# Gate and up projections of a decoder block by Strassen's seven products

## The chip, the cores and the metric

The kernel runs on one core of one Trainium2 chip. The metric is the device time of one execution in microseconds (us), the median of several runs. TensorE multiplies matrices, VectorE and ScalarE (in the rows DVE and ACT) work element by element, GpSimd is POOL, and SyncE (SP) issues the transfers from DRAM.

## The reference, cut to what matters

A decoder block with attention and convolution branches is followed by a SwiGLU feed-forward layer and a final norm, for 512 tokens of width 1,024; `D_FF` is 2,816. The change is in the feed-forward layer:

```python
    x = x + merged @ w_out
    h = rms_norm(x, norm_ffn_g)
    x = x + (jax.nn.silu(h @ w_ffn_gate) * (h @ w_ffn_up)) @ w_ffn_down
return rms_norm(x, norm_final_g)
```

All in float32.

## The kernel before

Every product of this part is made of three: each float32 operand is split into `hi`, its value rounded to the type F32R that TensorE takes, and `lo`, the rest, and `mm3` adds hi x hi, hi x lo and lo x hi into one PSUM bank. The weights are split on the fly. `wload` fetches two k tiles of 128 rows x 256 columns in one transfer of 256 KB (256 columns of float32, 1,024 bytes a row) into a tile `wr`; ScalarE casts it to `wh` (L136), and in this part VectorE subtracts to `wl` (L137). The pool of weights has six buffers each of `wr`, `wh` and `wl`, 128 x 512 elements a buffer.

The normalized input h is held transposed, channels on the partitions, as eight pairs `h2_hi[k]`, `h2_lo[k]` of 128 x 512 (channels x tokens). `h2_T` makes them for one half of the tokens at a time: TensorE transposes, ScalarE writes hi (L1034), VectorE writes lo (L1035).

Gate and up go chunk by chunk: eleven chunks of 256 columns of the 2,816. `ffn_chunk` does, for gate and then for up, two column halves m of 128, each with eight k tiles, with the weights as the stationary operand and 512 tokens as the moving one. At the end of a gate half ScalarE takes Silu out of PSUM (tile `sil`, L1059); at the end of an up half VectorE multiplies (L1065), ScalarE casts to `a_hi` (L1066) and VectorE subtracts to `a_lo` (L1067). Chunk 0 is done in two halves of 256 tokens, so that it can begin before the second half of h is transposed.

The down projection (tile `pd`) reads `a_hi` and `a_lo` as stationary operands, with `w_ffn_down` loaded by `wload_wide` (L147 to L149): first the left 512 output columns, all 22 k tiles for four token tiles; then the right 512, where the last `nl` = 8 k tiles are done token tile by token tile, each followed by its norm and its store.

A planner (the Tile framework) orders the instructions of each engine at compile time: among those that its own timing finds ready, the one that stands earlier in the program goes first. So the order on an engine can differ from that of the program, and is fixed in the compiled kernel. `tile_pool` hands out buffers by tag, `bufs` of each; an instruction that writes a buffer waits until the last reader of its former content is done.

Of the kernel before, what the change touches and what calls it, by code (L numbers as in the profile page):

```python
# [19 lines left out]
D = 1024  # L20
# [16 lines left out]
def hybrid_block(  # L37
# [72 lines left out]

    WG = 2

    def wload_raw(src, k0, nk, c0, ncol):

        pieces = []
        for a in range(0, nk, WG):
            n = min(WG, nk - a)
            raw = wp.tile([128, WG, 256], F32, name="wr", tag="wr", bufs=6)
# [6 lines left out]
    def wload(src, k0, nk, c0, ncol, pieces=None, on_dve=None, tile=None):  # L125

        on_dve = phase["lo_dve"] if on_dve is None else on_dve
        eng = nc.vector if on_dve else nc.gpsimd
        tile = tile or (lambda name: wp.tile([128, WG, 256], F32R, name=name, tag=name))
        res = []  # L130
        for raw, n in pieces or wload_raw(src, k0, nk, c0, ncol):
            hi, lo = tile("wh"), tile("wl")
            st = n if phase["early"] else min(n, 2)
            for a in range(0, n, st):
                sl = slice(a, min(a + st, n))
                nc.scalar.copy(hi[:, sl, :ncol], raw[:, sl, :ncol])  # L136
                eng.tensor_sub(lo[:, sl, :ncol], raw[:, sl, :ncol], hi[:, sl, :ncol].bitcast(F32))  # L137
            res += [(hi[:, j, :], lo[:, j, :]) for j in range(n)]
        return res

    def wload_wide(src, k, c0, ncol=512, parts=()):

        wide = [wp.tile([128, WG, 256], dt, name=n, tag=n, bufs=6 if n == "wr" else None)
                .rearrange("p a b -> p (a b)") for n, dt in (("wr", F32), ("wh", F32R), ("wl", F32R))[:3 - len(parts)]]
# [869 lines left out]

    hp = ctx.enter_context(tc.tile_pool(name="hid", bufs=16))
    for t in range(2, NT):
# [10 lines left out]

    def h2_T(th, hh):
        for k in range(KT):
            p = trp("th2")  # L1030
            for j in range(2):
# [19 lines left out]
    gfin = fp.tile([128, D], F32, name="gfin")  # L1051
    nc.gpsimd.dma_start(gfin, norm_final_g[None, :].to_broadcast([128, D]))

    def ffn_chunk(c, n0, n1):
        sgs = []

        def ev_g(m, p):
            s_ = fp.tile([128, S], F32, name="sil", tag="sil", bufs=3)
            nc.scalar.activation(s_[:, n0:n1], p[:, n0:n1], AF.Silu)  # L1059
            sgs.append(s_)  # L1060

        def ev_u(m, p):
            f = 2 * c + m
            s_ = sgs[m][:, n0:n1]
            nc.vector.tensor_mul(s_, p[:, n0:n1], s_)  # L1065
            nc.scalar.copy(a_hi[f][:, n0:n1], s_)  # L1066
            nc.vector.tensor_sub(a_lo[f][:, n0:n1], s_, a_hi[f][:, n0:n1].bitcast(F32))  # L1067

        for src, ev in ((w_ffn_gate, ev_g), (w_ffn_up, ev_u)):
            p = [dense("pf") for _ in range(2)]  # L1070
            for kh in range(2):
                ws = wload(src, 4 * kh, 4, 256 * c, 256)
                for m in range(2):
                    for kk in range(4):
# [31 lines left out]

    nl = 8
    pd = [dense("pd") for _ in range(NT)]
# [61 lines left out]
```

## Time and profile before

| | us |
|---|---|
| median of 3 runs (lowest to highest) | 971.59 (970.38 to 972.0) |
| profiled execution, its own time | 974.84 |
| its span, first to last instruction | 973.1 |
| TensorE busy | 940.4 (97%) |
| VectorE busy | 633.1 (65%) |
| ScalarE busy | 545.1 (56%) |
| gate and up chunks | from 601.8 to 845.3 |
| down projection to the end | from 845.3 to 973.1 |

The device time is that of the whole execution and is a little over the span. Busy times are sums of the durations on an engine; matmuls overlap each other, so their rate is read from their starts.

### The profile page before, as it was taken

What the parts mean: (1) busy time and instruction counts of PE and PEld (TensorE: products, weight loads), DVE (VectorE), ACT (ScalarE), POOL (GpSimd) and SP (SyncE); (2) the same over time, 40 slices, a digit from 0 to 9 for tenths busy, and PEclk for the clock granted to TensorE, in tenths of its full rate; (3) what the DMA queues carried; (4) which work ended last, traced back from release to release, by engine and by line L of the source; (5) the groups of instructions that cost most, each with busy time, mean ns of one, the idle gap of its engine ahead of it and who ended that gap; (6) DMA issues with size and microseconds to landing.
All of it is one profiled execution on the core that took longest, in us unless ns stands there. A gap on an engine that the chain in (4) does not pass through costs nothing.

```text
span 973.1 us, 14959 instructions
## 1 busy us (share of the span) xinstructions
PE 940.4 (97%) x5306; PEld 797.5 (82%) x5306; DVE 633.1 (65%) x1254; ACT 545.1 (56%) x1273; POOL 234.9 (24%) x256
## 2 busy tenths in 40 slices
PE   5999989899999999989999999999999999999996
PEld 5889979888888977877778878988888888888886
DVE  6799999987999987676876877633333343322512
ACT  6533545558879887999984776533333333322412
POOL 3545447853353342622322000000000000000000
PEclk9999989999999999999999999999999999999999
DMA  7333324542121111111212166633333323322302
GB/s 225 90 106 88 87 72 121 134 109 55 45 66 44 34 45 44 44 33 55 98 56 76 59 201 188 180 96 100 91 105 88 107 87 108 97 96 95 118 29 87
DMA packets 77599, 89.03 MB, mean 91 GB/s; under 512 B 5896, under 2 KB 65620, under 8 KB 77524
## 3 DMA queue, kind: packets, MB, share of 16 engines
q1 hardware_dynamic: 76676, 87.38, 30.0%
q8 instruction: 42, 0.69, 0.3%
q0 software_dynamic: 144, 0.52, 0.2%
q14 instruction: 33, 0.27, 0.1%
q10 hardware_dynamic: 704, 0.17, 0.1%
HBM read 85.96 MB, written 2.10 MB: 90 GB/s over the span
## 4 chain that ended last, share of the span: by engine, by line
PE 85%; DVE 7%; ACT 4%; issue 1%; DMA 1%; POOL 1%; SPq 0%; POOLq 0%; ACTq 0%; DVEq 0%
PE pf L211 8%; PE pf L212 8%; PE pf L213 8%; PE pch L213 7%; PE pch L211 7%; PE pch L212 7%; PE ptk L211 4%; PE ptk L212 4%; PE ptk L213 4%; PE pd L211 4%; PE pd L213 4%; PE pd L212 4%; PE tP L732 3%; PE sc L700 2%; PE sc L701 2%; PE pv L756 2%
## 5 line engine op out<-in xcount | busy, mean ns | idle before, releaser
L137 POOL TENSOR_TENSOR wl<-wr,wh 128x512 fp32r<-128x512 f32 x128 | 167.2, 1318 | 229.8 <-ACT wh L136 179.5
L136 ACT CAST wh<-wr 128x512 fp32r<-128x512 f32 x228 | 140.1, 622 | 145.0 <-PE pf L212 52.6
L794 DVE SCALAR_TENSOR_TENSOR cacc<-z,cw,cacc 128x512 f32<-128x512 f32 x232 | 165.5, 748 | 3.8 <-ACT cacc L792 1.7
L211 PE MATMUL pf<-h2hi,wh 128*128 128x512 f32 (+1 forms) x384 | 142.3, 372 | 0.6 <-ACT h2hi L1034 0.6
L212 PE MATMUL pf<-h2lo,wh 128*128 128x512 f32 (+1 forms) x384 | 142.5, 372 | 0.0
L213 PE MATMUL pf<-h2hi,wl 128*128 128x512 f32 (+1 forms) x384 | 142.4, 372 | 0.0
L137 DVE TENSOR_TENSOR wl<-wr,wh 128x512 fp32r<-128x512 f32 x100 | 68.7, 689 | 109.6 <-ACT wh L136 108.1
L213 PE MATMUL pch<-hThi,wl 128*128 128x512 f32 (+1 forms) x272 | 107.3, 395 | 1.5 <-POOL wl L137 1.5
L211 PE MATMUL pch<-hThi,wh 128*128 128x512 f32 (+1 forms) x272 | 107.3, 396 | 1.2 <-ACT hThi L195 1.2
L212 PE MATMUL pch<-hTlo,wh 128*128 128x512 f32 (+1 forms) x272 | 107.5, 396 | 0.0
L149 DVE TENSOR_TENSOR wl<-wr,wh 128x512 fp32r<-128x512 f32 x76 | 51.6, 689 | 61.9 <-ACT wh L148 61.8
L148 ACT CAST wh<-wr 128x512 fp32r<-128x512 f32 (+1 forms) x84 | 50.1, 604 | 73.7 <-PE pd L213 50.9
L708 ACT ACTIVATE P<-sc,nm 128x32 f32<-128x32 f32 (+3 forms) x192 | 84.7, 446 | 11.2 <-DVE nm L705 9.2
L1136 POOL TENSOR_TENSOR rstd<-rstd,half 128x1 f32<-128x1 f32 x4 | 2.2, 547 | 359.6 <-DVE rstd L1135 359.6
L211 PEld LDWEIGHTS pf<-h2hi,wh 128*128 128x128 f32 x384 | 72.0, 188 | 13.2 <-ACT h2hi L1034 0.8
L211 PE MATMUL ptk<-wh,hThi 128*128 128x256 f32 x288 | 82.7, 287 | 0.0
L213 PEld LDWEIGHTS pf<-h2hi,wl 128*128 128x128 f32 x384 | 72.2, 188 | 12.6
L212 PEld LDWEIGHTS pf<-h2lo,wh 128*128 128x128 f32 x384 | 72.2, 188 | 12.4
L212 PE MATMUL ptk<-wl,hThi 128*128 128x256 f32 x288 | 81.2, 282 | 0.0
L213 PE MATMUL ptk<-wh,hTlo 128*128 128x256 f32 x288 | 81.0, 281 | 0.0
L705 DVE TENSOR_REDUCE nm<-sc 128x1 f32<-128x32 f32 (+3 forms) x192 | 68.8, 381 | 16.8 <-PE sc L703 15.5
L211 PE MATMUL pd<-wh,ahi 128*128 128x512 f32 (+1 forms) x184 | 70.0, 380 | 0.8 <-DVE x L1092 0.8
(234 smaller groups left out, 2133.0 us busy)
## 6 DMA issues: line engine op xcount, KB each, us to landing
wr<-in_w_in_dram SPq DMA_DIRECT2D x100, 256.0 KB, 2.8
wr<-in_w_ffn_gate_dram SPq DMA_DIRECT2D x48, 256.0 KB, 2.7
wr<-in_w_ffn_up_dram SPq DMA_DIRECT2D x48, 256.0 KB, 2.7
wr<-in_w_ffn_down_dram SPq DMA_DIRECT2D x44, 256.0 KB, 2.5
wr<-in_w_out_dram SPq DMA_DIRECT2D x32, 256.0 KB, 2.6
x<-in_x_dram SPq DMA_DIRECT2D x8, 512.0 KB, 5.0
wr<-in_w_conv_out_dram SPq DMA_DIRECT2D x16, 256.0 KB, 2.7
wr<-in_cmp_k_w_dram SPq DMA_DIRECT2D x8, 256.0 KB, 2.6
```

Of the source, the lines that this page charges most:

```text
L136: nc.scalar.copy(hi[:, sl, :ncol], raw[:, sl, :ncol])
L137: eng.tensor_sub(lo[:, sl, :ncol], raw[:, sl, :ncol], hi[:, sl, :ncol].bitcast(F32))
L148: nc.scalar.copy(hi, raw)
L149: (nc.vector if phase["lo_dve"] else nc.gpsimd).tensor_sub(lo, raw, hi.bitcast(F32))
L211: nc.tensor.matmul(o, lh, rh, start=first, stop=False, skip_group_check=True)
L212: nc.tensor.matmul(o, lh, rl, start=False, stop=False, skip_group_check=True)
L213: nc.tensor.matmul(o, ll, rh, start=False, stop=last, skip_group_check=True)
L700: nc.tensor.matmul(sc[:, :e - a], qh[:, tsl], K[:, a:e], start=True, stop=False)
L705: nc.vector.tensor_reduce(out=nm[:, b:b + 1], in_=sc[:, ba - a:be - a], axis=AX.X, op=OP.max, negate=True)
L708: nc.scalar.activation(P[:, ba:be], sc[:, ba - a:be - a], AF.Exp, bias=nm[:, b:b + 1], accum_out=Dn[:, b, hh:hh + 1])
L732: nc.tensor.transpose(t4[:, 256 * b + 128 * hh:256 * b + 128 * hh + 128], Ps[hh][:, key_blk(j, b)], idn)
L794: nc.vector.scalar_tensor_tensor(cts[c] if j == TAPS - 1 else a, z[:, j:j + S], cw[:, j, c:c + 1], a, op0=OP.mult, op1=OP.add)
```

## The change

Chunks 2 to 10 are no longer done by `ffn_chunk` but by `pair`, which uses Strassen's scheme in the form of Winograd: a product of two by two blocks takes seven products of blocks and some sums. The blocks of the weights are the k halves (512 rows) by the column halves (128 columns) of a chunk, gate and up side by side in a tile `quad` of 128 x 1,024: a11, a12, a21, a22. The blocks of h are k halves by token halves of 256. The four sums of weights (s1 to s4) are made on VectorE before the split into hi and lo. The four combinations of h (t1 to t4) are made once, in `combine`, during chunks 0 and 1. A product is 24 matmuls of 256 columns: gate in the left half of a PSUM bank, up in the right one. The results are put together with additions on VectorE (`total`) and copies out of PSUM on ScalarE (`saved`).

Other edits: the hidden activations are kept in float32 (`a_`), and their split into hi and lo moves into the first half of the down projection; the full float32 h (`full`) and the combinations live in tiles of `a_` that are written late; after chunk 1 the pool of weights is closed and opened again with three buffers each of `wh`, `wl` and `ws`, twice as large; `gfin` is loaded after the pairs; `nl` goes from 8 to 5; `pd` takes two of its banks from another tag.

The diff, its core:

```diff
-    hp = ctx.enter_context(tc.tile_pool(name="hid", bufs=16))
+    hp = ctx.enter_context(tc.tile_pool(name="hid", bufs=32))
...
+            if full:
+                nc.scalar.activation(full[k][:, sl], p[:, :256], AF.Copy, scale=g_ffn[:, k:k + 1])
...
-    a_hi = [fp.tile([128, S], F32R, name=f"ahi{f}") for f in range(FT)]
-    a_lo = [fp.tile([128, S], F32R, name=f"alo{f}") for f in range(FT)]
+    def a_tile(name, dt=F32):
+        return fp.tile([128, S], dt, name=name, tag="A", bufs=FT + 1)
+
+    a_ = [a_tile(f"a{f}") for f in range(FT)]
...
+    full, comb = a_[6:14], a_[14:22]
+    quads = ctx.enter_context(tc.tile_pool(name="quads", bufs=3))
...
-            s_ = fp.tile([128, S], F32, name="sil", tag="sil", bufs=3)
+            s_ = fp.tile([128, S], F32, name="sil", tag="saved", bufs=2)
...
-            nc.vector.tensor_mul(s_, p[:, n0:n1], s_)
-            nc.scalar.copy(a_hi[f][:, n0:n1], s_)
-            nc.vector.tensor_sub(a_lo[f][:, n0:n1], s_, a_hi[f][:, n0:n1].bitcast(F32))
+            nc.vector.tensor_mul(a_[2 * c + m][:, n0:n1], p[:, n0:n1], sgs[m][:, n0:n1])
...
+    tok0, tok1 = slice(0, 256), slice(256, 512)
+    side = {"b11": [(h2_hi[k][:, tok0], h2_lo[k][:, tok0]) for k in range(4)],
+            "b21": [(h2_hi[k][:, tok0], h2_lo[k][:, tok0]) for k in range(4, 8)],
+            "b22": [(h2_hi[k][:, tok1], h2_lo[k][:, tok1]) for k in range(4, 8)]}
+
+    def combine(ns):
+        cb_ = [[comb[2 * n + kk // 2][:, 256 * (kk % 2):256 * (kk % 2) + 256] for kk in range(4)] for n in range(4)]
+        f11, f21 = ([full[k][:, tok0] for k in ks] for ks in (range(4), range(4, 8)))
+        f12, f22 = ([full[k][:, tok1] for k in ks] for ks in (range(4), range(4, 8)))
+        for n, (u, v) in enumerate(((f12, f11), (f22, cb_[0]), (f22, f12), (f21, cb_[1]))):
+            if n not in ns:
+                continue
+            for kk in range(4):
+                if n % 3 == 0:
+                    k = kk + n // 3 * 4
+                    nc.vector.tensor_add(full[k][:, tok0], h2_hi[k][:, tok0].bitcast(F32), h2_lo[k][:, tok0].bitcast(F32))
+                nc.vector.tensor_sub(cb_[n][kk], u[kk], v[kk])
+            parts = []
+            for j in range(2):
+                hi, lo = (hp.tile([128, S], F32R, name=f"t{n}{x}", tag="H") for x in "hl")
+                nc.scalar.copy(hi, comb[2 * n + j])
+                nc.vector.tensor_sub(lo, comb[2 * n + j], hi.bitcast(F32))
+                parts += [(hi[:, h_], lo[:, h_]) for h_ in (tok0, tok1)]
+            side[f"t{n + 1}"] = parts
+
+    def pair(c):
+
+        def quad(kh, m):
+            q = (hp.tile([128, 4, 256], F32, name="quad", tag="h2", bufs=2) if kh else
+                 quads.tile([128, 4, 256], F32, name="quad", tag="quad", bufs=3))
+            for x, src in enumerate((w_ffn_gate, w_ffn_up)):
+                nc.sync.dma_start(
+                    q[:, 2 * x:2 * x + 2, :].rearrange("p a (b n) -> p (a b) n", n=128),
+                    src[512 * kh:512 * kh + 512, 256 * c + 128 * m:256 * c + 128 * m + 128].rearrange(
+                        "(k p) n -> p k n", p=128))
+            return q
+
+        def split(q):
+            hi, lo = wtile("wh"), wtile("wl")
+            nc.scalar.copy(hi, q)
+            nc.vector.tensor_sub(lo, q, hi.bitcast(F32))
...
+        def diff(q, r, op=OP.subtract):
+            d = wp.tile([128, 4, 256], F32, name="ws", tag="ws", bufs=3)
+            nc.vector.tensor_tensor(d, q, r, op=op)
+            return d
+
+        def product(bank, w, name, first=True):
+
+            for x in range(2):
+                for kk in range(4):
+                    mm3(bank[:, 256 * x:256 * x + 256], w[0][:, x, kk, :], w[1][:, x, kk, :], *side[name][kk],
+                        first and x == kk == 0, kk == 3)
...
+        def total(u, v, name="sum"):
+            t_ = fp.tile([128, 512], F32, name=name, tag=name, bufs=2 if name == "sum" else 1)
+            nc.vector.tensor_add(t_, u, v)
+            return t_
+
+        def saved(u):
+            t_ = fp.tile([128, 512], F32, name="saved", tag="saved", bufs=2)
+            nc.scalar.copy(t_, u)
+            return t_
+
+        def out(t_, m, tok):
+            nc.scalar.activation(t_[:, 0:256], t_[:, 0:256], AF.Silu)
+            nc.vector.tensor_mul(a_[2 * c + m][:, tok], t_[:, 256:512], t_[:, 0:256])
+
+        a11, a21 = quad(0, 0), quad(0, 1)
+        a22, a12 = quad(1, 1), quad(1, 0)
+        X, Y, Z = bank("sc"), bank("dense"), bank("tr")
+        Q = bank(("cv", "pv")[c % 2], 1)
+        product(X, split(a11), "b11")
+        product(Y, split(a12), "b21")
+        s1 = diff(a21, a22, OP.add)
+        out(total(saved(X), Y), 0, tok0)
+        s2 = diff(s1, a11)
+        product(X, split(s2), "t2", False)
+        product(Z, split(s1), "t1")
+        s3 = diff(a11, a21)
+        v = saved(X)
+        u = total(v, Z, "part")
+        product(Y, split(s3), "t3")
+        s4 = diff(a12, s2)
+        out(total(u, Y), 1, tok1)
+        product(Q, split(s4), "b22")
+        out(total(u, Q), 0, tok1)
+        product(Y, split(a22), "t4", False)
+        out(total(v, Y), 1, tok0)
+
     ffn_chunk(0, 0, 256)
-    h2_T(1, hh)
-    ffn_chunk(0, 256, 512)
-    for c in range(1, DFF // 256):
-        ffn_chunk(c, 0, 512)
+    h2_T(1, hh, full)
+    ffn_chunk(0, 256, 512, ((), (0,), (), ()))
+    ffn_chunk(1, 0, 512, ((1,), (2,), (3,)))
+    wstack.close()
+    wp = ctx.enter_context(tc.tile_pool(name="weights2", bufs=3, side="right"))
+    size.update(wg=4, bufs=3, wr="ws")
+    for c in range(2, DFF // 256):
+        pair(c)
+    gfin = wp.tile([128, 4, 256], F32, name="gfin", tag="ws", bufs=3).rearrange("p a b -> p (a b)")
+    nc.gpsimd.dma_start(gfin, norm_final_g[None, :].to_broadcast([128, D]))
...
-    pd = [dense("pd") for _ in range(NT)]
+    pd = [trp("pd"), trp("pd"), dense("pd"), dense("pd")]
+    a_hi, a_lo = [], []
     for k in range(FT):
+        a_hi.append(hp.tile([128, S], F32R, name="ahi", tag="H"))
+        a_lo.append(a_tile("alo", F32R))
+        nc.scalar.copy(a_hi[k], a_[k])
+        nc.vector.tensor_sub(a_lo[k], a_[k], a_hi[k].bitcast(F32))
         wh, wl = wload_wide(w_ffn_down, k, 0)
...
-    nl = 8
+    nl = 5
```

## Rows read from the trace of the kernel before

**Rows 1.** The page: busy time of each engine; the chain that ended last.

```profile
PE 940.4 (97%) x5306; PEld 797.5 (82%) x5306; DVE 633.1 (65%) x1254; ACT 545.1 (56%) x1273; POOL 234.9 (24%) x256
...
PE 85%; DVE 7%; ACT 4%; issue 1%; DMA 1%; POOL 1%; SPq 0%; POOLq 0%; ACTq 0%; DVEq 0%
```

**Rows 2.** Windows: first and second half of chunk 0, chunk 1, a steady chunk, down.

```profile
core 0: us, PE busy (x) PEld busy (x) DVE busy (x) ACT busy (x) POOL busy (x), PEclk, DMA share, GB/s
601.80:613.30 11.50, 11.50 (x97) 11.47 (x96) 8.68 (x15) 8.71 (x16) 2.23 (x3) 1.00 0.76 240
613.30:627.00 13.70, 13.12 (x109) 12.68 (x108) 9.83 (x20) 8.70 (x20) 0.00 (x0) 1.00 0.52 149
627.00:649.00 22.00, 22.00 (x102) 18.33 (x101) 7.91 (x14) 7.80 (x14) 0.00 (x0) 1.00 0.40 118
...
694.00:716.00 22.00, 22.00 (x99) 18.22 (x98) 8.37 (x13) 7.45 (x13) 0.00 (x0) 1.00 0.35 97
...
846.00:908.00 62.00, 62.00 (x275) 51.36 (x274) 19.99 (x33) 16.80 (x31) 0.00 (x0) 1.00 0.30 98
```

**Rows 3.** Waits of TensorE from 600 us on: total, times, longest.

```profile
PE pd L211 <- DVE x L1092: 0.8, 1, 0.8
PE pf L211 <- ACT h2hi L1034: 0.6, 1, 0.6
```

**Rows 4.** Timeline, TensorE, 512 columns: start, duration; first and last of 25.

```profile
839.64 0.39 PE L213 MATMUL pf<-h2hi,wl 128*128 128x512 f32 x1
...
845.08 0.39 PE L213 MATMUL pf<-h2hi,wl 128*128 128x512 f32 x1
```

**Rows 5.** Timeline, ScalarE: the first Silu of two chunks that follow each other.

```profile
701.34 0.60 ACT L1059 ACTIVATE sil<-pf 128x512 f32<-128x512 f32 x1 [2.28 <-PE pf L213]
...
723.10 0.60 ACT L1059 ACTIVATE sil<-pf 128x512 f32<-128x512 f32 x1 [2.28 <-PE pf L213]
```

**Rows 6.** Timeline, TensorE, 256 columns: first and last of 94.

```profile
602.05 0.28 PE L213 MATMUL pf<-h2hi,wl 128*128 128x256 f32 x1
...
613.20 0.28 PE L213 MATMUL pf<-h2hi,wl 128*128 128x256 f32 x1
```

**Rows 7.** Groups by line, weight loads of 601.8 to 613.3: count, busy us, mean ns.

```profile
L213 PEld LDWEIGHTS pf<-h2hi,wl 128*128 128x128 f32 x32 | 6.1, 192 | 0.0
```

**Rows 8.** Groups by line and shape, mean ns; two by tile, ns min/median/max.

```profile
L492 DVE TENSOR_TENSOR kclo<-kctmp,kchi x4: 1204/1220/1806, 139.2 to 165.8; 128x1024 fp32r<-128x1024 f32 x4
L1065 DVE TENSOR_TENSOR sil<-pf,sil 128x512 f32<-128x512 f32 x20 | 13.8, 691 | 16.5 <-PE pf L213 16.0
L1065 DVE TENSOR_TENSOR sil<-pf,sil 128x256 f32<-128x256 f32 x4 | 1.7, 421 | 0.4 <-PE pf L213 0.4
L491 ACT CAST kchi<-kctmp x4: 1047/1049/1054, 136.3 to 164.2; 128x1024 fp32r<-128x1024 f32 x4
L1059 ACT ACTIVATE sil<-pf 128x512 f32<-128x512 f32 x20 | 11.9, 595 | 22.8 <-PE pf L213 22.8
L1059 ACT ACTIVATE sil<-pf 128x256 f32<-128x256 f32 x4 | 1.5, 381 | 0.1
L1066 ACT CAST ahi<-sil 128x512 fp32r<-128x512 f32 x20 | 12.4, 622 | 33.3 <-DVE sil L1065 33.3
```

**Rows 9.** Timeline, VectorE, where two chunks meet.

```profile
713.60 0.69 DVE L1067 TENSOR_TENSOR alo<-sil,ahi 128x512 fp32r<-128x512 f32 x1 [0.69 <-ACT ahi L1066]
714.21 0.68 DVE L137 TENSOR_TENSOR wl<-wr,wh 128x512 fp32r<-128x512 f32 x1
714.94 0.69 DVE L1065 TENSOR_TENSOR sil<-pf,sil 128x512 f32<-128x512 f32 x1
```

**Rows 10.** The page, transfers: size each, median us to landing.

```profile
wr<-in_w_ffn_gate_dram SPq DMA_DIRECT2D x48, 256.0 KB, 2.7
wr<-in_w_ffn_up_dram SPq DMA_DIRECT2D x48, 256.0 KB, 2.7
wr<-in_w_ffn_down_dram SPq DMA_DIRECT2D x44, 256.0 KB, 2.5
```

**Rows 11.** Timeline, ScalarE: second transposition, first and last hi.

```profile
613.97 0.83 ACT L1034 ACTIVATE h2hi<-th,vec 128x256 fp32r<-128x256 f32 x2
...
619.23 0.93 ACT L1034 ACTIVATE h2hi<-th,vec 128x256 fp32r<-128x256 f32 x2
```

More of the change, by code (lines that the diff above doesn't have):

```diff
@@ L109, in load_x, with wtile @@
         nc.sync.dma_start(hs[t][:, :D], x2[t * 128:(t + 1) * 128, :])
-    WG = 2
+    size = {"wg": 2, "bufs": 6, "wr": "wr"}
+    def wtile(name, dt=F32R):
+        return wp.tile([128, size["wg"], 256], dt, name=name, tag=size.get(name, name), bufs=size["bufs"])
     def wload_raw(src, k0, nk, c0, ncol):
         pieces = []
-        for a in range(0, nk, WG):
-            n = min(WG, nk - a)
-            raw = wp.tile([128, WG, 256], F32, name="wr", tag="wr", bufs=6)
+        for a in range(0, nk, size["wg"]):
+            n = min(size["wg"], nk - a)
+            raw = wtile("wr", F32)
             r0 = (k0 + a) * 128
@@ L123, in wload_raw, with wload @@
         return pieces
-    def wload(src, k0, nk, c0, ncol, pieces=None, on_dve=None, tile=None):
+    def wload(src, k0, nk, c0, ncol, pieces=None, on_dve=None):
         on_dve = phase["lo_dve"] if on_dve is None else on_dve
         eng = nc.vector if on_dve else nc.gpsimd
-        tile = tile or (lambda name: wp.tile([128, WG, 256], F32R, name=name, tag=name))
         res = []
         for raw, n in pieces or wload_raw(src, k0, nk, c0, ncol):
[L132 to L135, printed above, removed]
+            hi, lo = wtile("wh"), wtile("wl")
+            for a in range(0, n, 2):
+                sl = slice(a, min(a + 2, n))
                 nc.scalar.copy(hi[:, sl, :ncol], raw[:, sl, :ncol])
@@ L141, in wload_wide @@
     def wload_wide(src, k, c0, ncol=512, parts=()):
-        wide = [wp.tile([128, WG, 256], dt, name=n, tag=n, bufs=6 if n == "wr" else None)
-                .rearrange("p a b -> p (a b)") for n, dt in (("wr", F32), ("wh", F32R), ("wl", F32R))[:3 - len(parts)]]
+        wide = [wtile(n, dt).rearrange("p a b -> p (a b)")
+                for n, dt in (("wr", F32), ("wh", F32R), ("wl", F32R))[:3 - len(parts)]]
         wide += list(parts)
@@ L1026, in h2_norm, with h2_T @@
             nc.vector.tensor_scalar(h, x1[t], r, None, op0=OP.mult)
-    def h2_T(th, hh):
+    def h2_T(th, hh, full=None):
         for k in range(KT):
@@ L1046, in hybrid_block, with ffn_chunk @@
     fp = ctx.enter_context(tc.tile_pool(name="ffn", bufs=1))
-    a_hi = [fp.tile([128, S], F32R, name=f"ahi{f}") for f in range(FT)]
-    a_lo = [fp.tile([128, S], F32R, name=f"alo{f}") for f in range(FT)]
+    def a_tile(name, dt=F32):
+        return fp.tile([128, S], dt, name=name, tag="A", bufs=FT + 1)
+    a_ = [a_tile(f"a{f}") for f in range(FT)]
     hh = [hp.tile([128, D], F32, name="h2", tag="h2", bufs=2) for j in range(2)]
     h2_norm(1, hh)
-    gfin = fp.tile([128, D], F32, name="gfin")
-    nc.gpsimd.dma_start(gfin, norm_final_g[None, :].to_broadcast([128, D]))
-    def ffn_chunk(c, n0, n1):
+    full, comb = a_[6:14], a_[14:22]
+    quads = ctx.enter_context(tc.tile_pool(name="quads", bufs=3))
+    def ffn_chunk(c, n0, n1, between=()):
         sgs = []
         def ev_g(m, p):
-            s_ = fp.tile([128, S], F32, name="sil", tag="sil", bufs=3)
+            s_ = fp.tile([128, S], F32, name="sil", tag="saved", bufs=2)
             nc.scalar.activation(s_[:, n0:n1], p[:, n0:n1], AF.Silu)
@@ L1072, in ffn_chunk @@
                 ws = wload(src, 4 * kh, 4, 256 * c, 256)
+                at = 2 * (src is w_ffn_up) + kh
+                if at < len(between) and between[at]:
+                    combine(between[at])
                 for m in range(2):
@@ new lines, in pair, with bank @@
+    def pair(c):
[9 more added lines that the diff above has]
+        def split(q):
+            hi, lo = wtile("wh"), wtile("wl")
+            nc.scalar.copy(hi, q)
+            nc.vector.tensor_sub(lo, q, hi.bitcast(F32))
+            return [t_.rearrange("p (x a) (b n) -> p x (a b) n", x=2, n=128) for t_ in (hi, lo)]
+        def diff(q, r, op=OP.subtract):
[7 more added lines that the diff above has]
+                        first and x == kk == 0, kk == 3)
+        def bank(tag, bufs=2):
+            return ps.tile([128, 512], F32, name="pw", tag=tag, bufs=bufs)
+        def total(u, v, name="sum"):
[30 more added lines that the diff above has]
+        out(total(v, Y), 1, tok0)
```

5 lines of the change are left out of this document (2 added, 3 removed).

## The prediction

> **What bounds the kernel now.** I read the page first. TensorE is busy for 97% of the span, and the chain that ended last is 85% TensorE; VectorE is busy 65%, ScalarE 56% [rows 1]. These are means over unlike stages, so I then read the stage that the change touches, by windows. In a steady stretch of gate and up work TensorE has no idle time, VectorE works 8.4 of 22.0 us and ScalarE 7.5, at full granted clock [rows 2]. The view of waits says the same: from 600 us on only two waits of TensorE are listed, 1.4 us together [rows 3]. The reader is to see that this stage is set by TensorE alone and that the two vector engines have much room there.
>
> Next come the matmul starts, because a matmul's own duration (0.39 us) overlaps its neighbour's. With 512 columns, 24 matmuls take 845.08 - 839.64 = 5.44 us, 0.2267 us from start to start [rows 4]. A whole chunk is 2 matrices x 2 column halves x 8 k tiles x 3 terms = 96 matmuls, 96 x 0.2267 = 21.76 us, and two Silu instructions that stand one chunk apart are 723.10 - 701.34 = 21.76 us apart [rows 5]. With 256 columns, as in the first half of chunk 0, 93 matmuls take 613.20 - 602.05 = 11.15 us, 0.1199 us each [rows 6]. Half the width costs 53% of the time and not 50%.
>
> **TensorE's part.** A changed chunk (a pair, in the diff) has 7 products x 2 matrices x 4 k tiles x 3 terms = 168 matmuls of 256 columns: 168 x 0.12 = 20.16 us. The saving is 21.76 - 20.16 = 1.60 us a chunk and 9 x 1.60 = 14.4 us in all. The eighth product alone would be 21.76 / 8 = 2.72 us a chunk, 24.5 us in all; 10 us of it go to the narrower matmuls.
>
> Every narrow matmul has its own weight load. In the 256-column stretch the loads' row is busy 11.47 of 11.50 us [rows 2] and a load lasts 192 ns [rows 7], yet matmuls start every 120 ns, so most of each load lies beside matmuls. [...]
>
> **VectorE's part.** Per pair: seven splits and four sums or differences of 128x1024, five additions of two 128x512 tiles, four products of 128x256. The nearest rows are 1.220 us (128x1024 subtraction, two SBUF sources), 0.691 us (128x512, one source in PSUM) and 0.421 us (128x256) [rows 8]. 11 x 1.22 + 5 x 0.69 + 4 x 0.42 = 13.4 + 3.5 + 1.7 = 18.6 us. Back to back, starts are closer than that: 0.61 us between an alo and the wl behind it, each 0.68 to 0.69 [rows 9], so some 17.0 us of queue time is the lower bound and 18.6 the upper. VectorE thus goes from 8.4 of 22 us to 17.0 to 18.6 of 20.2.
>
> **ScalarE's part.** Seven casts at 1.05, two PSUM copies at 0.6 (the 128x512 Silu out of PSUM), four Silu at 0.38 [rows 8]: 7.4 + 1.2 + 1.5 = 10.1 us of 20.2. It has room.
>
> **Does the chain keep up?** One product takes 24 x 0.12 = 2.88 us. There are three buffers for split weights, so the split for product n+3 may begin when product n ends and is due two products, 5.76 us, later. It needs the cast, 1.05, and the subtraction, 1.22, together 2.3 us; 3.4 us are left for standing in VectorE's queue. None of the sums of weights needs a matmul's result: s1 to s4 need only transfers and buffers, so they can fill VectorE's gaps. The additions that empty PSUM must be done before the next product into the same bank: X is copied while product 2 runs, Y is read while products 3 and 6 run, 2.88 us for work of 0.69. Behind each addition that waits for TensorE stand the subtractions for later products, with those 3.4 us of slack. I take 0.25 us of TensorE waiting a pair, 2.3 us in all, near the lower bound, nothing, because TensorE waits so little today [rows 3]; the upper bound is the rival below.
>
> **Transfers.** Eight of 256 KB a chunk stay eight, but their rows in DRAM are 512 bytes and not 1,024. Today they land 2.7 us after issue while the DMA engines are busy for 35% [rows 2, 10]. If a packet costs the same at half its size, the share doubles to some 70% and landing nears 5.4 us. The last weight block of a pair to be freed is a22, split in product 5's time; the transfer that takes its place lands before the next pair's second product needs it, over 8 us later. I cost it at nothing; the cover is those 8 us.
>
> **The way in.** The second transposition (h2_T) gets eight further 128x256 ScalarE instructions, and the PSUM bank is held for them. Its eight today run from 613.97 to 620.16 us at 0.47 or less each [rows 11]; eight more end it up to 3.5 us later, while TensorE has the first halves of gate and up to do, 2 x 2.88 us. I take 1.5 us of waiting, between 0 and 3.5. The combinations of activations (24 pieces of 128x256, 8 splits of 128x512) are 24 x 0.42 + 8 x 0.69 = 15.6 us of VectorE spread over chunks 0 and 1, which leave it some 4 + 14 us idle [rows 2]: hidden, nearly all. When the weights pool changes, the first split can find its buffers still held by chunk 1. Then cast and subtraction stand open, 2.3 us; if old buffers go free one by one, nothing. I take 1.5.
>
> **The way out.** The hi and lo split of the hidden tiles moves from the chunks to the down projection: per k tile one cast more and one subtraction more, 0.62 and 0.69 us beside 12 x 0.2267 = 2.72 us of matmuls, with VectorE at 20 of 62 us there [rows 2, 8]: hidden. Fewer buffers for the down weights (three for six, and gfin holds one raw one) still leave a turn of 2.5 (landing) + 0.62 + 0.69 = 3.8 us against two k tiles, 5.4 us: hidden, 1.6 us of cover. The last eight k tiles done token tile by token tile become five, which shortens nothing on TensorE: 0, plus or minus 0.5.
>
> **Sum.** -14.4 + 2.3 + 1.5 + 1.5 = -9.1 us. The profiled execution took 974.84 us (span 973.1), 965.7 after the change; against the median of the runs, 971.59, this gives 962.5. I say 962.
>
> **Rivals.** *VectorE in program order (slower).* If the planner puts the instructions of a pair on VectorE as the program lists them, s2 and the split of s2 stand behind the addition after product 2 and the product with its Silu. From product 2's end that is 0.69 + 0.38 + 0.42 + 1.22 + 1.05 + 1.22 = 5.0 us before product 3 has both halves of its weights, some 4.5 us of TensorE idle; a pair is 24.7 us, 9 x 2.9 = 26 us more, with the way in about 1,001 us. A milder form, with half the idle, ends at 980. It turns from gain to loss at (14.4 - 3.0) / 9 = 1.3 us of waiting a pair. For it: VectorE is busy for 84 to 92% of a pair, so an order that is a little wrong can't be made up. Against it: today's order is not that of the program; a subtraction for the next chunk's weights stands between the alo of one column half and the product (sil) of the other [rows 9]. 19%.
>
> *Late transfers or a costlier way in (gain mostly gone).* If a22 or a12 comes 1 us late in each pair, 9 us are lost: 968 to 975, on both sides of no change. For it, 512-byte rows, of which this trace has no stage; against it, the 8 us of cover. 11%.
>
> *Weight loads not hidden (slower).* If each load stood in front of its matmul, the 72 further loads a pair at 0.192 us [rows 7] would cost 13.8 us against the 1.6 saved, 9 x 12.2 = 110 us: some 1,081. The 93 starts at 0.12 us speak against it. 2%. [...]
>
> **How the numbers follow.** Forecast (TensorE stays the bound, small waits): 68%, its own range 956.5 (nothing lost, 0.5 gained at the end) to 968. With the partial case (11%) the range to 976 holds 79%, and the mildest of the slow cases a little more: 956 to 976. A change below 0.2%, 1.9 us, can't be told from none here. Faster: 68 + 4 = 72%; same: 5%; slower: 23%.
>
> **What would show it.** Right: a pair's Silu instructions repeat every 20.2 to 20.6 us; 256-column matmuls start 0.12 us apart; VectorE is busy 17 to 18.6 us of a pair; waits of TensorE on wl are under 0.5 us a pair. Wrong: TensorE waits on wh or wl after product 2 or 4, with an addition (sum) ahead of that subtraction in VectorE's queue; a start to start of 256 columns above 0.125 us while VectorE is nearly full, which no stretch of this trace tests; casts that wait for a transfer; a gap of over 3 us at the change of pools.

## The result and the profile after

The changed kernel takes 961.54 us (median of 4 runs, 958.29 to 963.13) beside 971.8 us of the kernel before on the same chip: a ratio of 0.9882 [0.9863, 0.9902]. The forecast was 962 us. Timed again with five runs on another chip it took 963.35 us, 0.9868 [0.9846, 0.9889]. The profiled execution took 962.3 us, its span 960.6.

The page after, in the parts of [rows 1]: busy time of each engine, and the chain that ended last.

```profile
PE 925.8 (96%) x5945; PEld 814.0 (85%) x5945; DVE 738.4 (77%) x1374; ACT 585.9 (61%) x1314; POOL 237.1 (25%) x256
...
PE 83%; DVE 8%; ACT 4%; DMA 1%; issue 1%; POOL 1%; SPq 0%; POOLq 0%; ACTq 0%; DVEq 0%
```

TensorE works 14.6 us less, VectorE 105 us more, and the span is still TensorE's. Windows of the changed kernel (columns as in [rows 2]): second half of chunk 0, chunk 1, two pairs.

```profile
613.30:628.00 14.70, 14.17 (x114) 13.13 (x113) 13.82 (x32) 12.54 (x29) 0.00 (x0) 1.00 0.81 248
628.00:650.40 22.40, 22.40 (x98) 17.89 (x96) 11.69 (x25) 6.39 (x12) 0.00 (x0) 1.00 0.03 9
673.80:693.60 19.80, 19.80 (x171) 19.80 (x170) 18.61 (x23) 10.29 (x15) 0.00 (x0) 1.00 0.37 107
713.40:733.20 19.80, 19.80 (x170) 19.80 (x170) 17.25 (x21) 9.95 (x14) 0.00 (x0) 1.00 0.37 108
```

In a pair TensorE has no idle time, though VectorE works 17.25 to 18.61 of 19.80 us. The combinations of activations lie in the first two rows, where VectorE is busy 13.82 of 14.70 and 11.69 of 22.40 us. The waits of TensorE from 560 us on, the view of [rows 3]:

```profile
PE pw L214 <- ACT wh L1131: 1.6, 2, 1.2
PE pw L216 <- DVE wl L1132: 0.8, 1, 0.8
PE pw L214 <- DVE sum L1152: 0.5, 1, 0.5
PE pf L214 <- ACT h2hi L1037: 0.5, 1, 0.5
PE pd L214 <- DVE x L1202: 0.5, 1, 0.5
```

The first two lines lie at the change of pools, the third in the first pair. The other eight pairs have none. The timeline there, first where pools change, then in the first pair:

```profile
650.19 0.40 PE L216 MATMUL pf<-h2hi,wl 128*128 128x512 f32 x1
650.66 2.00 ACT L1131 CAST wh<-quad 128x1024 fp32r<-128x1024 f32 x2 [10.58 <-PE pf L216]
...
651.76 0.39 PE L214 MATMUL pw<-h2hi,wh 128*128 128x256 f32 x1 [1.18 <-ACT wh L1131]
...
652.71 0.39 PE L214 MATMUL pw<-h2hi,wh 128*128 128x256 f32 x1 [0.45 <-ACT wh L1131]
...
654.05 0.39 PE L216 MATMUL pw<-h2hi,wl 128*128 128x256 f32 x1 [0.84 <-DVE wl L1132]
...
668.78 1.22 DVE L1137 TENSOR_TENSOR ws<-quad 128x1024 f32<-128x1024 f32 x1 [1.38 <-DMA quad<-in_w_ffn_up_dram]
...
669.92 0.68 DVE L1152 TENSOR_TENSOR sum<-part,pw 128x512 f32<-128x512 f32 x1
...
670.75 0.36 PE L214 MATMUL pw<-t3h,wh 128*128 128x256 f32 x1 [0.54 <-DVE sum L1152]
```

The two casts at 650.66 (one row) begin when the last matmul of chunk 1, at 650.19, lets a buffer go. At 668.78 VectorE had waited 1.38 us for the transfer of a22 before it made s1; the addition behind it empties a bank 0.54 us late, and the next product waits for that bank.

What wasn't forecast is the pace of the narrow matmuls. Timeline of TensorE, two pairs of starts:

```profile
656.10 0.28 PE L215 MATMUL pw<-h2lo,wh 128*128 128x256 f32 x1
...
664.94 0.28 PE L214 MATMUL pw<-t2h,wh 128*128 128x256 f32 x1
...
679.65 0.28 PE L214 MATMUL pw<-t1h,wh 128*128 128x256 f32 x1
...
681.42 0.28 PE L214 MATMUL pw<-t1h,wh 128*128 128x256 f32 x1
```

The first two rows are 78 matmuls apart, 8.84 / 78 = 0.1133 us each; the last two 15, 0.118 each. The pace changes at the wait at 670.75 and stays at 0.1177 to the end of the pairs: 168 x 0.1177 = 19.77 us. Chunk 0 has both paces too: 0.1177 in its first half, 0.1133 at the end of its second, with waits between. By tile, the first and last of the nine additions `part`, one a pair, give the same mean, (824.3 - 665.6) / 8 = 19.84 us:

```profile
L1152 DVE TENSOR_TENSOR part<-saved,pw x9: 679/682/684, 665.6 to 824.3; 128x512 f32<-128x512 f32 x9
```

Where the 12.5 us between the two spans come from, by starts of TensorE's matmuls in the two timelines:

| stretch | before, us | after, us | difference |
|---|---|---|---|
| up to gate and up | 601.83 | 601.96 | +0.1 |
| chunk 0 | 25.85 | 26.07 | +0.2 |
| chunk 1, to the next weights | 21.77 | 23.73 | +2.0 |
| chunks 2 to 10 | 195.85 | 180.18 | -15.7 |
| down projection | 120.92 | 121.75 | +0.8 |

The profiled executions lay 3.0 us (before) and 0.8 us (after) above the medians of their runs; between medians 10.3 us remain.

### The profile page after: what moved, and what is told of

Same layout as the page of the kernel before. It is cut to its first block, busy times and chain, and to the rows that moved or that the text cites. A ratio compares the mean times of both kernels' runs of the same rounds, so it can differ in the third digit from the quotient of the medians.

```text
span 960.6 us, 16384 instructions
## 1 busy us (share of the span) xinstructions
PE 925.8 (96%) x5945; PEld 814.0 (85%) x5945; DVE 738.4 (77%) x1374; ACT 585.9 (61%) x1314; POOL 237.1 (25%) x256
## 3 DMA queue, kind: packets, MB, share of 16 engines
q1 hardware_dynamic: 95108, 87.38, 30.7%
## 4 chain that ended last, share of the span: by engine, by line
PE 83%; DVE 8%; ACT 4%; DMA 1%; issue 1%; POOL 1%; SPq 0%; POOLq 0%; ACTq 0%; DVEq 0%
PE pch L216 7%; PE pch L214 7%; PE pch L215 7%; PE pw L214 6%; PE pw L216 6%; PE pw L215 6%; PE pd L215 4%; PE pd L214 4%; PE ptk L214 4%; PE ptk L215 4%; PE ptk L216 4%; PE pd L216 4%; PE tP L735 3%; PE sc L703 2%; DVE cacc L797 2%; PE sc L704 2%
## 5 line engine op out<-in xcount | busy, mean ns | idle before, releaser
L139 ACT CAST wh<-wr 128x512 fp32r<-128x512 f32 x156 | 95.5, 623 | 61.5 <-PE pch L215 23.4
L152 DVE TENSOR_TENSOR wl<-wr,wh 128x512 fp32r<-128x512 f32 x76 | 51.8, 689 | 69.3 <-ACT wh L151 69.2
L215 PE MATMUL pd<-wl,ahi 128*128 128x512 f32 (+1 forms) x181 | 70.2, 388 | 0.0
L739 DVE TENSOR_TENSOR ptl<-tP,pth 128x512 fp32r<-128x512 f32 x80 | 54.8, 686 | 20.1 <-ACT pth L738 19.0
L216 PE MATMUL pd<-wh,alo 128*128 128x512 f32 (+1 forms) x181 | 69.2, 382 | 0.0
L726 ACT ACTIVATE P<-P,R 128x128 f32<-128x128 f32 (+3 forms) x128 | 62.5, 560 | 7.5 <-DVE R L721 6.5
L214 PE MATMUL pw<-h2hi,wh 128*128 128x256 f32 x216 | 60.8, 281 | 1.6 <-ACT wh L1131 1.6
L216 PE MATMUL pw<-h2hi,wl 128*128 128x256 f32 x216 | 60.5, 281 | 0.8 <-DVE wl L1132 0.8
L215 PE MATMUL pw<-h2lo,wh 128*128 128x256 f32 x216 | 60.6, 280 | 0.0
L216 PEld LDWEIGHTS pch<-hThi,wl 128*128 128x128 f32 x272 | 52.0, 191 | 9.2 <-POOL wl L140 1.8
```

What stands on the lines that cost most here:

```text
L214: nc.tensor.matmul(o, lh, rh, start=first, stop=False, skip_group_check=True)
L215: nc.tensor.matmul(o, lh, rl, start=False, stop=False, skip_group_check=True)
L216: nc.tensor.matmul(o, ll, rh, start=False, stop=last, skip_group_check=True)
L726: nc.scalar.activation(P[:, ba:be], P[:, ba:be], AF.Copy, scale=R[:, b, hh:hh + 1])
L739: nc.vector.tensor_sub(pl, t4, ph.bitcast(F32))
```

## The experiments

Twelve runs; "before" took 973.6 to 977.3 us beside them. Diffs are against the changed kernel unless they name the kernel before.

**again.** The changed kernel, five runs and a second profile.

> The changed kernel once more, unaltered. In its first profile the start to start of 256-column matmuls was 0.1133 us until TensorE's wait of 0.5 us in the first pair, and 0.1177 us after it to the end of the pairs, although the instructions are the same. Theory A: the rate is set anew when TensorE has waited and holds until its next wait, so another execution can show another level (0.1133, 0.1177 or 0.12) in pairs 2 to 9, and runs of the same kernel differ by up to 168 x 9 x 0.0067 = 10 us. Theory B: the rate belongs to the code of each stretch; then this profile shows 0.1133 and 0.1177 in the same places. Time against before: 0.986 to 0.990 by both.

963.35 us, 959.04 to 964.92. In the second profile the paces are the same at the same places: 512 columns at 0.2333 us in chunk 1, 256 columns at 0.1133 until a wait of 0.2 us for a sum in the first pair, 0.1177 from there. The drop followed a wait at that place both times; it isn't scatter of one profile. One thing differs. Behind the waits at the change of pools, which are the same in both profiles, the granted clock was 0.51 for 3.4 us here, and 1.00 in the first profile; its 16 matmuls start 0.213 us apart, some 1.6 us lost:

```profile
655.00:658.40 3.40, 3.36 (x15) 3.36 (x16) 3.40 (x4) 1.05 (x1) 0.00 (x0) 0.51 0.00 0
```

**eight_products.** All edits of the change but Strassen itself.

```diff
-        pair(c)
+        ffn_chunk(c, 0, S)
```

> Chunks 2 to 10 take eight products of 512 columns as before the change, all other edits stay (combinations of activations, pools, the split of the hidden tiles in the down projection, nl 5). Theory: the gain is TensorE's, from the seven products, and the other edits only cost. The profile before and after gives for chunks 2 to 10 195.9 and 180.2 us, and for the rest +3 us. So this kernel takes 1 to 4 us more than before, 973 to 976. Rival: the gain comes from the lighter end of a chunk (cast and subtraction of the hidden tiles moved away); then it is faster than before by 3 us or more.

990.56 us, 1.0161 [1.0141, 1.0182]: well above the 973 to 976 us that I expected. The waits of TensorE show one of 4.9 us where the pools change:

```profile
PE pf L214 <- ACT wh L139: 4.9, 1, 4.9
```

and 512 columns at 0.2333 us in chunks 1 to 10 instead of 0.2267, 960 x 0.0067 = 6.4 us. Of the remaining 4 us, by starts, 1.0 lie in the down projection, 0.9 before chunk 1 and some 1.6 around the wait. Against this kernel seven products are worth 990.56 - 963.35 = 27.2 us: 9 x (96 x 0.2333 - 19.77) = 23.7, and 2.4 of the wait. Against the same kernel with eight products, leaving one out gains nearly its whole price, 22.4 / 8 = 2.8 us a chunk; the edits around it, with wide products, cost 16 us.

**narrow.** The kernel before, each gate and up product of 512 columns as two of 256.

```diff
-                    for kk in range(4):
...
+                    for q0 in range(n0, n1, 256):
+                        for kk in range(4):
...
```

> The kernel before, with every gate and up product of chunks 1 to 10 done as two matmuls of 256 columns in place of one of 512: eight products, only narrower. Theory as in the prediction: half the width costs 0.12 us and not 0.1133, so a chunk takes 192 x 0.12 = 23.04 us for 21.76, ten chunks 12.8 us more: 982 to 986. Rival: narrow matmuls cost just half (0.1133, as a part of the changed kernel shows); then 970 to 974, no change. In between, at 0.1177 us, 8.4 us more: 980.

988.94 us, 1.0137 [1.0123, 1.0151]. 256 columns stay at 0.12 us all through. 10 chunks x (192 x 0.12 - 21.76) = 12.8 us forecast. By starts the stage takes 256.3 us beside 243.5, 12.8 more; over the whole span it is 14.2, of which 1.4 lie before the stage, where the code is the same. In the kernel before the price of [rows 6] holds for the whole stage, not for chunk 0 alone.

**placed.** So width alone doesn't set the pace: 256 columns take 0.12 us in narrow, 0.1133 and 0.1177 in the changed kernel. The change also moves the weights: in its code both pools, the first one of chunks 0 and 1 too, lie at the other end of the on-chip memory (`side="right"`). The diff above shows this for the second pool alone. Here the kernel before, with its pool of weights put there (and opened one line later, behind `res`); every engine has the same instructions in the same order, only addresses differ. With the weights gone from their old place, the pools behind them, the tiles of h2 among them, move by the 36 KB a partition that their 18 buffers took by the code (18 x 512 x 4 bytes).

```diff
-    wp = ctx.enter_context(tc.tile_pool(name="weights", bufs=6))
...
+    wp = ctx.enter_context(tc.tile_pool(name="weights", bufs=6, side="right"))
```

> The kernel before, with its weights pool on the other side of SBUF, where the changed kernel has it; every engine's order of instructions is the same as before, only addresses differ. It tells apart why the kernel with eight products under the new pools ran its 512-column matmuls at 0.2333 us and not at 0.2267. Theory: the rate hangs on where the tiles lie; then chunks 1 to 10 here run at 0.2333, a chunk takes 22.4 us, ten of them 6.4 us more, the down projection up to 7 us more, 977 to 988 beside 972 to 975. Rival: it hangs on something else (the order, the waits of the engine); then 0.2267 from chunk 1 on and the time of before.

982.93 us, 1.0071 [1.0057, 1.0085]. Timeline of TensorE, the 24 matmuls of [rows 4]:

```profile
760.15 0.39 PE L213 MATMUL pf<-h2hi,wl 128*128 128x512 f32 x1
...
765.75 0.39 PE L213 MATMUL pf<-h2hi,wl 128*128 128x512 f32 x1
```

5.60 / 24 = 0.2333 us, against 0.2267 there, with the same waits of TensorE. 256 columns went the other way, from 0.12 to 0.1177 in the first half of chunk 0 and to 0.1133 in the second. With the addresses alone changed, the wide matmuls here take 6.6 ns more each and the narrow ones 2.3 to 6.7 less, and the time is 982.93 us in the median of four runs beside 975.70. Whether the place of the weights or that of h2 does it, this run doesn't tell.

**narrow_placed.** Both edits on the kernel before.

> Eight products of 256 columns as in the narrow kernel, with the weights pool on the side of SBUF where the changed kernel has it; the order of instructions is that of the narrow kernel. Theory from the placement run: where the weights lie sets the rate, and for 256 columns the far side is the faster one (0.1133 to 0.1177 us in the changed kernel, 0.12 in the narrow one). Then a chunk takes 192 x 0.1133 to 0.1177 = 21.75 to 22.6 us and not 23.04, ten chunks 4 to 13 us less than the narrow kernel, less some 3 us more in the down projection: ratio to before 1.003 to 1.012, where the narrow kernel had 1.0137. Rival: the rate in the pairs comes from something else; then 0.12 us and a ratio of 1.014 to 1.020.

Ten runs, median 975.90 us, 1.0032 [1.0004, 1.006], at two levels: six from 974.78 to 976.01 and four from 983.97 to 986.50. The profile fell on the upper one, with 256 columns at 0.1177 us. The levels are 10 us apart; 1,920 matmuls x (0.1177 - 0.1133) = 8.4 us would be the step from 0.1177 to 0.1133, but no profile of the lower level exists, so that is argued and not shown. What is shown is that one kernel has two levels of time from execution to execution, and that in this profile one pace holds for the 230 us from 621 to 854 us, in which TensorE never waits.

**program_order.** The slower rival made real: s2 may be issued on VectorE only after the product with the first Silu.

```diff
-            nc.vector.tensor_mul(a_[2 * c + m][:, tok], t_[:, 256:512], t_[:, 0:256])
+            return nc.vector.tensor_mul(a_[2 * c + m][:, tok], t_[:, 256:512], t_[:, 0:256]).ins
...
-        out(total(saved(X), Y), 0, tok0)
-        s2 = diff(s1, a11)
+        first = out(total(saved(X), Y), 0, tok0)
+        with tc.issue_after(first):
+            s2 = diff(s1, a11)
```

> The changed kernel with the second sum of weights (s2) tied on VectorE behind the addition and the product that follow on product 2: the order of the program, the prediction's slower rival. By the rival's price TensorE idles 4.5 us in each pair: 961.5 + 9 x 4.5 = 1,002. By the theory that the planner can fill part of it with product 4, which needs only s1: 4.7 us of chain less the 2.8 of product 4, 1.9 us a pair, 961.5 + 17 = 979. If VectorE's order doesn't matter: 961 to 963.

1,025.26 us, 1.0505 [1.0486, 1.0525]. VectorE's and then TensorE's timeline in one pair, then TensorE's waits in all and the window behind the wait shown:

```profile
689.75 0.43 DVE L1162 TENSOR_TENSOR a<-sum 128x256 f32<-128x256 f32 x1 [0.48 <-ACT sum L1161]
690.09 1.22 DVE L1137 TENSOR_TENSOR ws<-ws,quad 128x1024 f32<-128x1024 f32 x1
...
692.44 0.46 PE L214 MATMUL pw<-t1h,wh 128*128 128x256 f32 x1 [3.97 <-ACT wh L1131]
```

```profile
PE pw L214 <- ACT wh L1131: 40.9, 20, 5.8
```

```profile
692.40:696.00 3.60, 3.30 (x14) 3.00 (x15) 3.60 (x5) 1.88 (x2) 0.00 (x0) 0.53 0.62 184
```

s2 (690.09) stands behind the product (689.75), and TensorE waits 3.97 us for its cast. The mechanism is real, 62 us more than the changed kernel beside it, 963.35. It costs more than the prediction's 1,001 us, though the waits are near its price: 40.9 us less the 1.6 at the change of pools, 4.4 a pair beside 4.5. What the price lacked is the granted clock behind the waits, 0.53 in the window. Some 200 of the 1,512 narrow matmuls stand in such stretches and start 0.213 us apart, which by their starts costs some 16 us; the mean granted clock is 0.965.

**sums_twice** and **two_sums_twice.** How much room has VectorE? Every sum of weights, s1 to s4, is made twice (4.9 us more a pair); then only s3 and s4 (2.4 us more; its diff).

```diff
-        def diff(q, r, op=OP.subtract):
+        def diff(q, r, op=OP.subtract, n=1):
...
-            nc.vector.tensor_tensor(d, q, r, op=op)
+            for _ in range(n):
+                nc.vector.tensor_tensor(d, q, r, op=op)
...
-        s3 = diff(a11, a21)
+        s3 = diff(a11, a21, n=2)
...
-        s4 = diff(a12, s2)
+        s4 = diff(a12, s2, n=2)
```

> The changed kernel with each of the four sums of weights of a pair made twice: 4 x 1.14 us more for VectorE in each pair, nothing else. By the trace VectorE has 17.1 us of work in a pair of 19.8. Theory: VectorE has 2.7 us to spare and becomes the bound beyond that, so a pair takes 21.7 us, 9 x 1.9 = 17 us more: 978 to 984, with VectorE busy all the time in the pairs. Rival: what holds a pair up is not VectorE's sum but the chain from a freed buffer over cast and subtraction; then the time rises by less than 5 us, below 968.

> The changed kernel with two of the four sums of weights of a pair (s3 and s4) made twice: 2 x 1.14 = 2.3 us more for VectorE in each pair, 19.4 us of 19.8. With four made twice a pair took 24.2 us, 2.5 more than VectorE's own sum. Theory: VectorE's room in a pair can be used nearly to the end, and only past it the waits come; then 0 to 0.5 us a pair more, 961 to 968. Rival: the order on VectorE leaves no room, an instruction more delays those behind it by its whole length; then 1 to 2.3 us a pair more, 971 to 984.

Four twice: 1,001.35 us, 1.026 [1.0246, 1.0274]. Windows over two pairs, columns as before:

```profile
700.00:721.00 21.00, 18.44 (x141) 17.83 (x140) 18.50 (x21) 8.31 (x11) 0.00 (x0) 0.92 0.35 101
721.00:747.50 26.50, 24.25 (x200) 23.04 (x200) 24.84 (x29) 10.88 (x15) 0.00 (x0) 1.00 0.27 80
```

VectorE is busy 43.34 of 47.50 us and TensorE idles 4.8: TensorE is no longer the bound of a pair. VectorE idles too, so it is its chain, and not its sum alone; the time lies above both expectations. Two twice: 970.26 us, 0.9944 [0.9927, 0.996], 7 us over the changed kernel and between the two expectations. Its waits of TensorE name the low half of the weights:

```profile
PE pw L216 <- DVE wl L1132: 7.0, 12, 1.1
```

Of 2.4 us put on VectorE a pair, the time shows 0.8; of 4.9, 4.2 (38 us / 9), a part of it at a lower granted clock (0.92 in the first window). But 0.8 is too little: with two twice most narrow matmuls run at 0.1133 us, beside 0.1177 in the changed kernel, and that hides a part of the loss. Beside a22_ahead (below), whose pairs run at 0.1133 too, the pairs take 187.5 us for 174.9, 1.4 us each. So about 1 us of work a pair still found room on VectorE, and hardly more.

**no_combinations.** What the way in costs: `full` and t1 to t4 are not made, and the products that use them read tiles of h2 instead.

> The changed kernel without the making of the four combinations of h: full, comb and their splits are left out, and the products read h2 tiles in their place. It measures what the way in costs through VectorE and ScalarE. Theory: these are hidden, chunk 0 grew by 0.2 us and chunk 1 by 0.6 us (its rate) between the profiles; so 0 to 1.5 us faster than the changed kernel, 960 to 963.5. Rival: they cost what the prediction gave the way in, 1.5 us or more; then 957 to 960.

967.81 us, 0.9918 [0.9902, 0.9933]: slower than the changed kernel though it does less. From the first gate matmul to the first of a pair it takes 49.34 us beside 49.80, so the combinations cost 0.5 us. In the pairs the planner ordered VectorE otherwise, and TensorE waits for additions there:

```profile
PE pw L214 <- DVE sum L1152: 6.3, 6, 1.5
```

By starts, chunks 2 to 10 take 3.7 us more than in the changed kernel and the down projection 2.2 us more, at 0.2333 us a matmul for 0.229. So as a whole the run is inconclusive on the way in; the time lies above both expectations.

**first_split_early.** The first pair's split is made during chunk 1, in buffers that are idle there.

> The changed kernel, with the first pair's first split done during chunk 1, into a free quad buffer (hi) and the two buffers of the sums (lo), so that it need not wait for the pool of weights to change. In the profile TensorE waits 1.2 + 0.4 + 0.8 us there. Theory: the change of pools is the cause, and 2 to 2.5 us come back: 959 to 961.5 where the changed kernel takes 961.5 to 963.4, ratio to before about 0.985. If the second split then takes over the wait, 0 to 1 us comes back. If the rate of the narrow matmuls settles at 0.1133 us after it, because the waits fall elsewhere, up to 7 us more.

962.59 us, 957.62 to 963.33, 0.9849 [0.9829, 0.987]. The wait at the pools is gone, but the profile has a new one of 1.9 us before product 7 of the second pair: s1 of the next pair waits 2.67 us for a22's transfer, and the addition that empties the bank stands behind it. From there 256 columns run at 0.1177 for six pairs, so nothing is gained that can be told from the changed kernel. Timeline of TensorE: the first product, whose weights were split into buffers outside the second pool, then the wait, then a later product 7:

```profile
651.01 0.28 PE L214 MATMUL pw<-h2hi,wh 128*128 128x256 f32 x1
...
653.88 0.28 PE L214 MATMUL pw<-h2hi,wh 128*128 128x256 f32 x1
...
689.39 0.36 PE L214 MATMUL pw<-t3h,wh 128*128 128x256 f32 x1 [1.85 <-DVE sum L1155]
...
810.00 0.28 PE L215 MATMUL pw<-t3l,wh 128*128 128x256 f32 x1
...
828.83 0.28 PE L216 MATMUL pw<-h2hi,wl 128*128 128x256 f32 x1
```

The first two rows are 24 matmuls apart, 0.1196 us each, with the tiles of h2 where they are in every pair: that speaks for the place of the weights as what the pace went with, though in one product, and no wait stands before it. The last two are 166 apart, 0.1134: behind a gap of 0.2 us, before 809.80, the faster pace is back. So each pace was seen behind a gap.

**a22_ahead.** Takes away what that wait waits for: a12 gets a buffer of its own, and a22 both buffers, so that it is fetched a pair ahead.

```diff
-            q = (hp.tile([128, 4, 256], F32, name="quad", tag="h2", bufs=2) if kh else
+            q = (hp.tile([128, 4, 256], F32, name="quad", tag="h2", bufs=2) if kh and m else
+                 quads.tile([128, 4, 256], F32, name="quad", tag="q12", bufs=1) if kh else
```

> The changed kernel with one buffer more for weight blocks: a22 keeps the two buffers it shared with a12, a12 gets one of its own, so a22 can be fetched a whole pair ahead. In the profiles s1 waits on VectorE 1.3 to 2.7 us for the transfer of a22 in early pairs, the addition behind it is late, and TensorE waits 0.2 to 1.9 us before product 7. Theory (late transfers, a rival of the prediction): these waits go, 0.5 us at once; and if the wait is what takes the narrow matmuls from 0.1133 to 0.1177 us, pairs 2 to 9 take 19.04 us and not 19.78, 6 us more: 955 to 957 on the first chip's scale, ratio to before 0.980 to 0.983. Rival: the rate falls back anyway; then the gain is 0 to 1 us, ratio 0.986 to 0.988.

956.96 us, 956.72 to 958.27, 0.9814 [0.9802, 0.9827]: 4.6 and 6.4 us below the two medians of the changed kernel. Windows over two pairs, and `part` by tile:

```profile
670.00:689.04 19.04, 19.04 (x170) 19.04 (x169) 18.00 (x22) 10.02 (x13) 0.00 (x0) 1.00 0.37 110
700.00:719.04 19.04, 19.04 (x170) 19.04 (x170) 17.36 (x21) 9.91 (x13) 0.00 (x0) 1.00 0.38 111
```

```profile
L1153 DVE TENSOR_TENSOR part<-saved,pw x9: 679/682/683, 666.9 to 819.1; 128x512 f32<-128x512 f32 x9
```

No wait for a sum is left, and a pair takes (819.1 - 666.9) / 8 = 19.03 us = 168 x 0.1133 from the first to the last. VectorE does its 17.4 to 18.0 us in this shorter time too. TensorE's instructions and their order are those of the changed kernel, and so, by the code, are the addresses they read. Without the wait of 0.5 us the pace never fell in this profile; in the changed kernel's the late transfer cost 0.5 us by itself, and the pace that followed it 168 x 0.0044 x 8 = 6 us.

**early_and_ahead.** Both edits.

> The first split during chunk 1 and the buffer more for a22 together. Theory: both waits of TensorE in the first two pairs are gone, 2.5 us at the change of pools and 0.5 to 1.9 us before product 7: ratio to before 0.983 to 0.985 at 0.1177 us a matmul, 0.976 to 0.979 if all pairs run at 0.1133 us. Rival: the planner, with another buffer, orders VectorE otherwise and a new wait takes the place of the old: ratio 0.985 to 0.988.

The profiled execution took 953.32 us, the fastest profile here, with pairs of 19.1 us and 1.5 us of waits of TensorE from 560 us on. But six runs scatter from 952.57 to 962.25, median 958.95, 0.9823 [0.9792, 0.9853]. No profile of its slower executions exists, so whether they run at the other pace isn't shown. That interval overlaps the changed kernel's, 0.9868 [0.9846, 0.9889]; a22_ahead's does not, so a22_ahead is the version shown to beat both kernels.

## Why the prediction was right

The time, 961.54 against 962, and the mechanism are right: TensorE stays the bound, and VectorE's chain keeps up. The terms of the sum are less good than it, and their errors offset only in part: the profiles differ by 12.5 us and not by 9.1. That the median fell within 0.5 us of 962 is partly luck, the more so as the pace of the narrow matmuls, worth 6 us over the pairs, was 0.1177 us here and 0.1133 in a22_ahead. Between the two profiles:

| step | forecast, us | found, us |
|---|---|---|
| seven products, narrow | -14.4 | -17.5 |
| waits in the pairs | +2.3 | +0.5 |
| way in | +1.5 | +0.2 |
| change of pools | +1.5 | +2.5 |
| pace of chunk 1 and of the way out, and before the stage | 0 | +1.7 |
| sum | -9.1 | -12.6 |

- **TensorE's part** was mis-sized. I took 0.12 us a narrow matmul from chunk 0, with 1.60 us saved a pair; it was 0.1177, with 21.76 - 19.77 = 1.99, and 2.72 at the 0.1133 of a22_ahead, the whole eighth. "Half the width costs 53%" held with the tiles where the kernel before has them (0.12 us all through narrow) and not where placed has them (0.1177 and 0.1133), and I gave it to the width. What I named as a proof against it, a start to start above 0.125 us, did not come.
- **Weight loads** are hidden: the loads' row is busy 19.80 of 19.80 us, a load lasts 188 to 192 ns there, and matmuls start 0.113 to 0.118 us apart, load included.
- **VectorE's part**, 17.0 to 18.6 us, was 17.25 to 18.61. **ScalarE's**, 10.1, was 9.95 to 10.29.
- **The chain keeps up**: one wait of 0.5 us instead of 0.25 in each pair. That it keeps up is the planner's order and not mere room: with the order of the program the same work takes 1,025 us, and of 2.4 us more work in a pair more than half reaches TensorE.
- **The slower rival** did not come, but its mechanism is shown by program_order: its waits at the rival's price, its time above 1,001 by the granted clock behind them (0.53 in the window shown, 0.965 in the mean).
- **Transfers.** The share of the DMA engines did not double: 0.37 beside 0.35 [rows 2]. On the two pages queue q1 moves the same 87.38 MB in 95,108 packets instead of 76,676 and takes 30.7% of the engines' span instead of 30.0%, so by my estimate from these a packet of half the size cost about half here. A gate half landed in 3.0 us (the page's median). Yet the late a22 of the second rival is real: its up half was issued at 663.74 us and ended the wait of s1 at 668.78, 5.0 us later, where a transfer before the change landed in 2.7 [rows 10]. I costed it at nothing, with 8 us of cover counted to the next pair's second product; but VectorE takes up s1, and so waits for a22, before product 7 of the pair ahead (668.78). The direct cost was 0.5 us, and the pace that stood behind it 6 us; a price of 1 us in every pair was the wrong form.
- **The way in** cost 0.2 us in chunk 0, near the lower end of its range, nothing. A part is hidden by the faster narrow matmuls there (0.1177 and 0.1133 us instead of 0.12): beside placed, whose chunk 0 takes 25.3 us, it is 0.8. The combinations, by no_combinations, cost 0.5 over chunks 0 and 1.
- **The change of pools** cost 1.18 + 0.45 + 0.84 = 2.5 us, just over its upper bound of 2.3: the first split's buffers were held by chunk 1 to its last matmul.
- **The way out** took 0.8 us more, at 0.229 us a matmul instead of 0.2267. The edits I weighed there cost nothing that shows; the pace does, as in chunk 1 (96 x 0.0067 = 0.6 us).

What stays open: why the pace changed with the place of the tiles (0.2267 to 0.2333 us and 0.12 to 0.1177 and 0.1133 in placed), what decides which of the two narrow paces follows a wait, and why executions of one kernel differ. The profiles show this much: in none of them does the narrow pace change inside the pairs without a gap of TensorE, and behind gaps both paces occur. In the first profile, in again and at 689 us of first_split_early the slower one followed; at 810 us of first_split_early the faster one did, and in no_combinations, between waits for sums, 1,060 of 1,512 narrow matmuls run at the faster one and 428 at the slower. So in these profiles a wait alone didn't bring the pace down; a22_ahead shows that without that wait it stayed, in one profile and by the time in four runs.

## What to carry to other kernels

Take the price of an instruction from a stage whose operands lie where the new ones will lie, or keep both paces as bounds: here the place of the tiles alone was worth 7 us (placed, 982.93 beside 975.70). When a change fills an engine nearly to the length of a stage (VectorE 17.25 to 18.61 of 19.80 us here), read which instruction stands ahead of which in its queue, and give the one operand that comes late a buffer more; here that was worth some 5 us, ten times the wait that it took away. And run the edits around an idea without the idea: eight_products shows that seven products for eight were worth 27 us in this layout, of which 11 remained against the kernel before.

## What was not expected of the hardware

- With the same instructions in the same order and other addresses of the tiles, 512-column matmuls started 0.2333 us apart in placed and 0.2267 in the kernel before, 256-column ones 0.1177 and 0.1133 instead of 0.12 (placed, 1.0071 [1.0057, 1.0085]).
- In the pairs of the changed kernel 256 columns had two paces, 0.1133 us up to a wait of TensorE in the first pair and 0.1177 from there to the end of the pairs, in both of its profiles; narrow_placed has two levels of time, near 975 and 985 us, from run to run.
- Behind the same waits at the change of pools the granted clock was 1.00 in one profile of the changed kernel and 0.51 for 3.4 us in the other (again).
- Transfers with 512-byte rows moved 107 GB/s at a DMA share of 0.37, those with 1,024-byte rows 97 at 0.35 [rows 2]; the up half of a22 that s1 waited for came 5.0 us after its issue (663.74 to 668.78).
